# One kernel, one change: who makes the low half of a split weight tile in the mixer's input projections

## The chip, the cores and the metric

The kernel runs on one core of one Trainium2 chip. The metric is the time of one execution on the device in microseconds (us). Five engines work side by side and meet at semaphores: TensorE (PE in the profile; its weight loads are the row PEld), VectorE (DVE), ScalarE (ACT), GpSimd (POOL) and SyncE (SP). SP issues nearly all loads from DRAM; POOL issues a few transfers through a queue of its own. The transfers of all queues are carried by the core's 16 DMA engines.

## The reference: what is computed

A diffusion backbone of two layers over 256 latent and 256 context tokens of width 1024. All is float32. Each layer has three parts, each with its own RMS norm, shift, scale and gate:

```python
x = add_residual(x, swiglu(modulate(x, ...), ffn_w_in[l, 0], ffn_w_out[l, 0]), ...)
h = modulate(x, ...); hc = modulate(xc, ...)
rq, rk, rv, rg, dq, dk, dv, gates = jnp.split(h @ w_in, SPLIT_POINTS, axis=-1)   # same for hc
# retention heads from rq, rk, rv, rg; differential attention heads from dq, dk, dv
y = (g_a * ret_out + g_b * diff_out) @ w_out
x = add_residual(x, y, ...)
x = add_residual(x, swiglu(modulate(x, ...), ffn_w_in[l, 1], ffn_w_out[l, 1]), ...)
```

The change touches the product `h @ w_in`, which is 1024 x 8192 weights per layer. In the second layer the context tokens need only some of its columns, since their output is not used any more.

## The kernel before, in words

TensorE multiplies in a reduced format (float32r). To keep float32 accuracy every operand is split into a high half (the value rounded to float32r) and a low half (what the rounding left), and every product is three matmuls (`mm3`, lines 301 to 303): high times high, high times low, low times high. In the transposed projections (`projT`, `ps<-h,w` in the profile) a weight tile's low half is first read by line 303, in the plain ones (`proj`, `ps<-w,h`) by line 302. The matmul ahead of it needs the high half alone.

Weights come from DRAM as tiles of 128 x 1024 float32 (512 KB), issued by SP into a ring of four buffers (`rawp`, line 121). `split` (line 125) turns one such tile into a pair of halves in a ring of five buffers (`wp`): ScalarE writes the high half with a copy (line 128), VectorE writes the low half as source minus high half (line 129). A raw buffer is free again when both have read it; a `w` buffer is free when TensorE has done its last matmul with it.

The mixer of a layer (`mixer`) runs 32 projection blocks, each of 256 columns of `w_in` and thus of two weight tiles. `proj_w` loads and splits the two; `projT_c` and `proj_c` do the matmuls for the latent and the context tokens, 48 matmuls for each of the two. In the second layer 18 of the 32 blocks are for the latent tokens alone. A tile framework orders each engine's instructions at build time, puts the attention and retention work between the projections, and adds the semaphores. Each engine then runs its list strictly in order: an instruction that waits holds up all that stand behind it. Around the mixer stand the feed-forward stages (`ffn`) and the norms: `norm_xn` (line 248 scales by a factor from POOL, lines 232 to 235), `norm_q` (lines 259 to 267: transposes on TensorE, shift and scale on ScalarE). The evictions of the projections (`rotate`, `ev_diff`, lines 504 to 532) run on VectorE and ScalarE.

Of the kernel before, what the change touches and what calls it, by code (L numbers as in the profile page):

```python
# [12 lines left out]
F32R = mybir.dt.float32r  # L13
BF16 = mybir.dt.bfloat16
AF = mybir.ActivationFunctionType
ALU = mybir.AluOpType
AX = mybir.AxisListType

P = 128
# [13 lines left out]
def build(ctx, tc, a):  # L33
    nc = tc.nc
# [3 lines left out]
    pool = nc.gpsimd  # L38
# [4 lines left out]
    wp = ctx.enter_context(tc.tile_pool(name="wp", bufs=5))  # L43
# [73 lines left out]
    def load(src, halves=(0, 1), pl=rawp, nm="raw"):  # L117
        rs = []
        for j in halves:
            r = pl.tile([P, 1024], F32, tag=nm, name=nm)  # L120
            nc.sync.dma_start(r, src[:, j * 1024:(j + 1) * 1024])
            rs.append(r)
        return rs

    def split(src, pin=False):
        keep = tc.keep_in_program_order if pin else (lambda z: z)
        w = wp.tile([P, 2, 1024], F32R, tag="w", name="w")
        keep(nc.scalar.copy(w[:, 0, :], src))  # L128
        keep(dve.tensor_tensor(out=w[:, 1, :], in0=src, in1=w[:, 0, :], op=ALU.subtract))  # L129
        return w  # L130

    cs = {}
# [172 lines left out]
    def fin_w(l, i, f, halves=(0, 1), pin=False):  # L305
        return [split(r, pin) for r in load(a["fin"][l, i, f], halves)]
# [10 lines left out]
    def ffn(l, i, st, AB, fetch, pairs, side, nside, after=None, out=None):  # L317
# [51 lines left out]
        def fout_w(f2):  # L369
            r = load(a["fout"][l, i, f2])  # L370
            ws = [split(r[0]), split(r[1])]
            if f2 < NP - 2:
                gt = hp.tile([P, 2, 2, 512], F32R, tag="h", name="gs")
                gs = [gt[:, 0], gt[:, 1]]
            else:
                gs = [slot([P, 2, 512], F32R) for _ in range(2)]
            for j in range(2):
                gsrc = g[f2][:, j, :N]
                nc.scalar.copy(gs[j][:, 0, :N], gsrc)
                dve.tensor_tensor(out=gs[j][:, 1, :N], in0=gsrc, in1=gs[j][:, 0, :N], op=ALU.subtract)  # L380
            slots.put(g[f2])
            return ws, gs
# [30 lines left out]
    def mixer(l, st, AB, fetch, after):  # L413
# [42 lines left out]

        def proj_w(b):
            r = load(a["win"][l, b])
            return [split(r[0]), split(r[1])]

        def proj_c(ws, c, ev):
            b0 = bank()
# [14 lines left out]
        def proj(b, pairs, ev):  # L477
            ws = proj_w(b)
            for c in pairs:
                proj_c(ws, c, ev)  # L480

        def projT(b, pairs, ev):
            ws = proj_w(b)
            for c in pairs:
                projT_c(ws, c, ev)
# [303 lines left out]
        def diff_blocks(u):  # L789
            KH = [slot([P, 2, 512], F32R) for _ in range(2)]  # L790
            KL = [slot([P, 2, 512], F32R) for _ in range(2)]
            Q = [slot([P, 2, 512], F32R) for _ in range(2)]
            dv = slot([P, 4, 256])
            ek, eq = ev_diff(KH, KL), ev_diff(Q, None)
            if u == 0:
                wk, wq = proj_w(16), proj_w(12)
                projT_c(wk, LAT, ek)
                norm_pair(CTX, AB, h)
                projT_c(wq, LAT, eq)
                projT_c(wk, CTX, ek)  # L800
                if not last:
                    projT_c(wq, CTX, eq)
                K.update(mixer_consts())
            else:
                projT(16 + u, BOTH, ek)
                projT(12 + u, QP, eq)
            proj(20 + u, BOTH, ev_V(dv))
            flush()
            defer(f"d{u}", diff_attn(u, KH, KL, Q, dv), 2 * NQ + 3, 4 * NQ + LAG)
# [57 lines left out]
        def wo_w(u):  # L867
            r = load(a["wout"][l, u])
            return [split(r[0]), split(r[1])]
# [8 lines left out]
        for u in range(n0):  # L878
            w = wo_w(u)
# [3 lines left out]
        w = sum((wo_w(u) for u in range(n0, 4)), [])  # L883
# [145 lines left out]
```

## Time and profile before

| | |
|---|---|
| median of 3 runs | 2225.74 us (2221.16 to 2225.74) |
| the profiled execution's own time | 2223.86 us |
| its span in the profile | 2222.1 us |
| mean granted TensorE clock | 0.993 of full |
| TensorE busy | 2173.7 us (98%) |
| VectorE busy | 1381.6 us (62%) |
| ScalarE busy | 863.5 us (39%) |
| POOL busy | 130.7 us (6%) |
| first layer's mixer, projections | about 407 to 879 us |
| second layer's mixer, projections | about 1664 to 1994 us |

The share of an engine is an average over stages. What matters for a change in one stage is which wait ends last there, so the timeline of that stage is read beside the totals. Idle time of an engine that nobody waits for costs nothing.

### The profile page before, as it was taken

Reading aid. Unit: us, or ns where it says so; the run is one execution under the profiler, and the core shown is the slowest. Engines: PE = TensorE matmul, PEld = TensorE weight load, DVE = VectorE, ACT = ScalarE, POOL = GpSimd, SP = SyncE. Lnnn points to the kernel's source line nnn. Section 1 sums busy time; section 2 is a strip of 40 time slices with the busy share of each in tenths; the row PEclk is TensorE's granted clock in tenths of the full one; section 3 lists DMA queues with packets and bytes.
Section 4 is the critical chain, followed back from the end, with each engine's and each line's share of the span. In section 5 each row is a group of like instructions: output and inputs, shape, how many; then the busy total and the mean of one; then the engine's idle time right before and its main releaser. Section 6 shows DMA issues by size and latency. Waiting matters only on the chain. (4 is left out here: it accounts for less than half of the span.)

```text
span 2222.1 us, 32737 instructions
## 1 busy us (share of the span) xinstructions
PE 2173.7 (98%) x13190; PEld 1932.0 (87%) x13190; DVE 1381.6 (62%) x2240; ACT 863.5 (39%) x1379; POOL 130.7 (6%) x248
## 2 busy tenths in 40 slices
PE   7999999999999999999999999999999999998998
PEld 4888888899999999888888888888889999997997
DVE  3799542777767664587234269844348777767554
ACT  3322232645355432432233252223236545445443
POOL 1000000200100010200000020000010010001000
PEclk9999999999999999999999999999999999999999
DMA  9577432212122223266223227853213222345553
GB/s 339 188 253 251 168 114 95 69 68 80 66 77 77 81 84 115 77 212 217 102 95 133 95 100 255 293 187 114 95 64 109 103 88 101 129 154 180 187 184 133
DMA packets 85081, 307.31 MB, mean 138 GB/s; under 512 B 9969, under 2 KB 10049, under 8 KB 84929
## 3 DMA queue, kind: packets, MB, share of 16 engines
q1 hardware_dynamic: 81648, 295.73, 38.2%
q0 software_dynamic: 2848, 8.43, 1.4%
q8 instruction: 103, 1.69, 0.3%
q10 hardware_dynamic: 432, 1.06, 0.1%
q14 instruction: 50, 0.40, 0.1%
HBM read 304.10 MB, written 1.09 MB: 137 GB/s over the span
## 5 line engine op out<-in xcount | busy, mean ns | idle before, releaser
L129 DVE TENSOR_TENSOR w<-raw,w 128x1024 fp32r<-128x1024 f32 x408 | 497.3, 1221 | 461.4 <-ACT w L128 459.9
L301 PE MATMUL ps<-h,w 128*128 128x256 f32 (+1 forms) x2144 | 712.5, 334 | 3.2 <-DVE h L266 2.9
L302 PE MATMUL ps<-h,w 128*128 128x256 f32 (+1 forms) x2144 | 712.9, 333 | 0.0
L303 PE MATMUL ps<-h,w 128*128 128x256 f32 (+1 forms) x2144 | 712.1, 333 | 0.5 <-DVE w L129 0.5
L128 ACT CAST w<-raw 128x1024 fp32r<-128x1024 f32 x408 | 427.5, 1052 | 678.9 <-PE ps L303 606.1
L301 PEld LDWEIGHTS ps<-h,w 128*128 128x128 f32 x2144 | 407.6, 191 | 47.1 <-DVE h L266 7.3
L302 PEld LDWEIGHTS ps<-h,w 128*128 128x128 f32 x2144 | 408.3, 190 | 40.4 <-issue 0.8
L303 PEld LDWEIGHTS ps<-h,w 128*128 128x128 f32 x2144 | 407.8, 190 | 39.2 <-DVE w L129 1.1
L301 PE MATMUL ps<-w,h 128*128 128x256 f32 x1088 | 308.9, 284 | 0.0
L302 PE MATMUL ps<-w,h 128*128 128x256 f32 x1088 | 308.1, 283 | 0.0
L303 PE MATMUL ps<-w,h 128*128 128x256 f32 x1088 | 307.8, 283 | 0.0
L146 DVE CUSTOM_DVE_ANT_0 jd<-ada,r 128x1024 bf16<-128x1024 f32 x224 | 273.4, 1220 | 15.0 <-DMA ada<-wada_dram 10.0
L301 PEld LDWEIGHTS ps<-w,h 128*128 128x128 f32 x1088 | 208.6, 192 | 0.4
L302 PEld LDWEIGHTS ps<-w,h 128*128 128x128 f32 x1088 | 208.7, 192 | 0.3
L303 PEld LDWEIGHTS ps<-w,h 128*128 128x128 f32 x1088 | 208.6, 192 | 0.0
L301 PE MATMUL ps<-w,gs 128*128 128x512 f32 x504 | 196.2, 389 | 0.0
L302 PE MATMUL ps<-w,gs 128*128 128x512 f32 x504 | 196.1, 389 | 0.0
L303 PE MATMUL ps<-w,gs 128*128 128x512 f32 x504 | 196.1, 389 | 0.0
L330 ACT ACTIVATE t<-ps 128x512 f32<-128x512 f32 (+1 forms) x88 | 47.9, 544 | 252.7 <-PE ps L303 252.7
L331 DVE TENSOR_TENSOR r<-ps,t 128x512 f32<-128x512 f32 (+1 forms) x88 | 54.7, 622 | 94.5 <-PE ps L303 65.3
L301 PEld LDWEIGHTS ps<-w,gs 128*128 128x128 f32 x504 | 94.6, 188 | 19.7
L302 PEld LDWEIGHTS ps<-w,gs 128*128 128x128 f32 x504 | 94.6, 188 | 19.7
(172 smaller groups left out, 2171.5 us busy)
## 6 DMA issues: line engine op xcount, KB each, us to landing
raw<-fin_dram SPq DMA_DIRECT2D x176, 512.0 KB, 4.1
ada<-wada_dram SPq DMA_DIRECT2D x128, 512.0 KB, 4.8
raw<-win_dram SPq DMA_DIRECT2D x128, 512.0 KB, 3.6
raw<-fout_dram SPq DMA_DIRECT2D x88, 512.0 KB, 3.5
r<-wada_dram SPq DMA_DIRECT2D x16, 512.0 KB, 10.3
raw<-wout_dram SPq DMA_DIRECT2D x16, 512.0 KB, 3.6
r<-scr POOLq DMA_DIRECT2D x10, 512.0 KB, 4.6
r<-cc_dram SPq DMA_DIRECT2D x7, 512.0 KB, 5.8
```

The source lines that it names most:

```text
L128: keep(nc.scalar.copy(w[:, 0, :], src))
L129: keep(dve.tensor_tensor(out=w[:, 1, :], in0=src, in1=w[:, 0, :], op=ALU.subtract))
L146: dve.tensor_tensor_reduce(out=junk, in0=r[j], in1=cs[c], scale=1.0, scalar=0.0, op0=ALU.mult, op1=ALU.add, accum_out=out[:, c, 2 * u + j: ...
L301: mm(o, lhsT=wH, rhs=xH, start=start, stop=False)
L302: mm(o, lhsT=wH, rhs=xL, start=False, stop=False)
L303: mm(o, lhsT=wL, rhs=xH, start=False, stop=stop)
L330: act(sg[:, :N], ab[0][:, :N], AF.Silu)
L331: dve.tensor_tensor(out=g[f // 2][:, f % 2, :N], in0=ab[1][:, :N], in1=sg[:, :N], op=ALU.mult)
```

## The change

A second way to split is added and used for the weights of `w_in` alone. ScalarE writes the high half as before. ScalarE then writes the negated source, rounded the same way, into the low half's place. POOL issues a transfer from the raw tile onto the low half's place that adds: source plus the negated high half. VectorE has no part in these 128 tiles (64 in each layer). The tiles of the feed-forward stages and of `w_out` are split as before.

```diff
+    def split_acc(src):
+        w = wp.tile([P, 2, 1024], F32R, tag="w", name="w")
+        nc.scalar.copy(w[:, 0, :], src)
+        nc.scalar.mul(w[:, 1, :], src, -1.0)
+        pool.dma_start(w[:, 1, :], src, accum_op=ALU.add)
         return w
...
         def proj_w(b):
             r = load(a["win"][l, b])
-            return [split(r[0]), split(r[1])]
+            return [split_acc(r[0]), split_acc(r[1])]
```

Line numbers behind the new function are 7 higher in the changed kernel: 527 becomes 534, 232 becomes 239. The new instructions are lines 134 (copy), 135 (negated copy) and 136 (adding transfer).

The change moves instructions on three engines. First ScalarE in the second layer, at the second tile of a block that follows a block for the latent tokens alone (`w_15109` before, `w_15188` now; r and ps are the targets and sources of the evictions). Before:

```order
L527 CAST r12_14892<-ps5_14974 64x2x256
L128 CAST w_15109<-raw_15104 128x1024
L531 CAST r12_14892<-ps5_14974 64x2x256
L532 COPY r4_14894<-r4_14894 64x2x256
L527 CAST r13_14893<-ps5_14974 64x2x256
L128 CAST w_15216<-raw_15212 128x1024
```

Now:

```order
L534 CAST r12_14966<-ps5_15050 64x2x256
L134 CAST w_15188<-raw_15182 128x1024
L538 CAST r12_14966<-ps5_15050 64x2x256
L539 COPY r4_14968<-r4_14968 64x2x256
L534 CAST r13_14967<-ps5_15050 64x2x256
L135 ACTIVATE w_15188<-raw_15182 128x1024
L538 CAST r13_14967<-ps5_15050 64x2x256
```

The negated copy stands three evictions behind the copy of the same tile, where the next tile's copy stood before.

Second, ScalarE in the second layer some 130 us later (`w_16689` before, `w_16792` now). Before:

```order
L128 CAST w_16689<-raw_16684 128x1024
L527 CAST r1_16463<-ps4_16554 64x2x256
L527 CAST r1_16463<-t2_16538 64x2x256
L531 CAST r1_16463<-t2_16538 64x2x256
L527 CAST r2_16464<-t2_16538 64x2x256
```

Now:

```order
L134 CAST w_16792<-raw_16786 128x1024
L534 CAST r1_16561<-t2_16638 64x2x256
L538 CAST r1_16561<-t2_16638 64x2x256
L534 CAST r2_16562<-t2_16638 64x2x256
L539 COPY r4_16563<-r4_16563 64x2x256
L538 CAST r2_16562<-t2_16638 64x2x256
L539 COPY r14_16564<-r14_16564 64x2x256
L534 CAST r1_16561<-ps4_16654 64x2x256
L135 ACTIVATE w_16792<-raw_16786 128x1024
```

Here seven evictions stand between a tile's copy and its negated copy.

Third, POOL at the start of the first layer's mixer, where the factors of the norms are made (pm, pr). Before:

```order
L235 TENSOR_TENSOR pr_2905<-pm_2902,cneg_98 128x1
L232 TENSOR_SCALAR pm_2942<-ss_2933 128x1
L233 TENSOR_SCALAR pm_2942<-ss_2933,pm_2942 128x1
L235 TENSOR_TENSOR pr_2945<-pm_2942,cneg_98 128x1
L232 TENSOR_SCALAR pm_3047<-ss_3042 128x1
```

Now:

```order
L242 TENSOR_TENSOR pr_2905<-pm_2902,cneg_98 128x1
L239 TENSOR_SCALAR pm_2942<-ss_2933 128x1
L136 DMA w_2965<-raw_2959 128x1024
L240 TENSOR_SCALAR pm_2942<-ss_2933,pm_2942 128x1
L242 TENSOR_TENSOR pr_2945<-pm_2942,cneg_98 128x1
L136 DMA w_2973<-raw_2969 128x1024
L136 DMA w_2977<-raw_2971 128x1024
L239 TENSOR_SCALAR pm_3051<-ss_3046 128x1
```

Adding transfers stand among the norm factors, in the order in which their tiles are made.

## Rows read from the trace of the kernel before

**Rows 1.** The page, part 1: busy us (share), xinstructions, by engine.

```profile
PE 2173.7 (98%) x13190; PEld 1932.0 (87%) x13190; DVE 1381.6 (62%) x2240; ACT 863.5 (39%) x1379; POOL 130.7 (6%) x248
```

**Rows 2.** Stretches: length, busy by engine, granted clock, DMA share, GB/s.

```profile
1660.00:1990.00 330.00, 326.70 (x2626) 318.58 (x2626) 250.69 (x443) 174.09 (x288) 24.74 (x44) 1.00 0.33 111
430.00:880.00 450.00, 444.05 (x3599) 434.22 (x3598) 303.62 (x620) 200.83 (x377) 31.14 (x61) 1.00 0.24 81
2000.00:2050.00 50.00, 42.35 (x266) 38.81 (x266) 34.87 (x48) 26.86 (x43) 7.76 (x12) 0.90 0.51 177
400.00:450.00 50.00, 47.55 (x353) 45.55 (x352) 41.94 (x80) 33.60 (x61) 8.34 (x13) 0.97 0.26 88
```

**Rows 3.** Waits of PE: waited for, us in total, times, longest.

```profile
PE ps L259 <- DVE t L248: 16.5, 12, 6.2
...
PE ps L303 <- DVE w L129: 0.5, 2, 0.2
```

**Rows 4.** Groups: busy us, mean ns | idle before, releaser.

```profile
L129 DVE TENSOR_TENSOR w<-raw,w 128x1024 fp32r<-128x1024 f32 x408 | 497.3, 1221 | 461.4 <-ACT w L128 459.9
...
L128 ACT CAST w<-raw 128x1024 fp32r<-128x1024 f32 x408 | 427.5, 1052 | 678.9 <-PE ps L303 606.1
```

**Rows 5.** Timeline (start us, us, instruction, idle before), first layer, 829 to 846 us.

```profile
829.56 1.05 ACT L128 CAST w<-raw 128x1024 fp32r<-128x1024 f32 x1 [4.84 <-PE ps L303]
...
845.32 0.28 PE L302 MATMUL ps<-w,h 128*128 128x256 f32 x1
```

**Rows 6.** DMA queue q1 (packets, MB, share); issues (KB each, us to landing).

```profile
q1 hardware_dynamic: 81648, 295.73, 38.2%
...
raw<-win_dram SPq DMA_DIRECT2D x128, 512.0 KB, 3.6
...
r<-wada_dram SPq DMA_DIRECT2D x16, 512.0 KB, 10.3
...
r<-scr POOLq DMA_DIRECT2D x10, 512.0 KB, 4.6
```

**Rows 7.** Timeline, ACT and PE, second layer, 1739 to 1744 us.

```profile
1739.17 1.05 ACT L128 CAST w<-raw 128x1024 fp32r<-128x1024 f32 x1
...
1741.96 1.05 ACT L128 CAST w<-raw 128x1024 fp32r<-128x1024 f32 x1
...
1743.59 0.28 PE L302 MATMUL ps<-w,h 128*128 128x256 f32 x1
```

**Rows 8.** Timeline, ACT and PE, start of the first layer's mixer.

```profile
405.01 2.95 ACT L128 CAST w<-raw 128x1024 fp32r<-128x1024 f32 x3
...
408.91 0.39 PE L303 MATMUL ps<-h,w 128*128 128x256 f32 x1
```

**Rows 9.** Timeline, ACT and PE, second layer, 1871 to 1878 us.

```profile
1871.65 0.62 ACT L527 CAST r<-t 64x512 fp32r<-64x512 f32 x1 [0.81 <-DVE t L509]
...
1877.37 0.28 PE L302 MATMUL ps<-w,h 128*128 128x256 f32 x1
```

**Rows 10.** Timeline, ACT and PE, first layer, 433 to 439 us.

```profile
433.53 1.05 ACT L128 CAST w<-raw 128x1024 fp32r<-128x1024 f32 x1 [6.65 <-PE ps L303]
434.48 1.26 ACT L527 CAST r<-t 64x512 fp32r<-64x512 f32 x2
435.76 0.58 ACT L527 CAST r<-ps 64x512 fp32r<-64x512 f32 x1
...
438.37 0.28 PE L302 MATMUL ps<-w,h 128*128 128x256 f32 x1
```

**Rows 11.** Timeline, ACT and PE, second layer, 1680 to 1685 us.

```profile
1681.73 2.85 ACT L263 ACTIVATE t<-ps,adaB,adaA 128x256 f32<-128x256 f32 x6
...
1680.12 0.28 PE L302 MATMUL ps<-w,h 128*128 128x256 f32 x1
```

**Rows 12.** Timeline, PE: two places where it stood [idle before <-releaser].

```profile
424.66 0.50 PE L301 MATMUL ps<-h,w 128*128 128x256 f32 x2 [1.77 <-DVE h L266]
...
2022.23 1.09 PE L259 MATMUL ps<-ident,t 128*128 128x128 f32 x4 [6.15 <-DVE t L248]
```

More of the change, by code (lines that the diff above doesn't have):

```diff
@@ L129, in split @@
         keep(dve.tensor_tensor(out=w[:, 1, :], in0=src, in1=w[:, 0, :], op=ALU.subtract))
+        return w
+    def split_acc(src):
[3 more added lines that the diff above has]
+        pool.dma_start(w[:, 1, :], src, accum_op=ALU.add)
         return w
```

## The prediction

> **What bounds the kernel now.** I read the shares of the engines first: TensorE is busy for 98% of the span, VectorE for 62%, ScalarE for 39% and POOL for 6% [rows 1]. Next come the stretches of the two mixers: in 430 to 880 us TensorE is idle for 450 - 444.05 = 5.95 us, in 1660 to 1990 us for 330 - 326.7 = 3.3 us, at the full granted clock [rows 2]. So in the stages that change, TensorE sets the pace, and all that could be won by making its operands sooner is some 9 us. The waits of TensorE say the same: it waited for VectorE's low half of a weight tile twice, 0.5 us in all; its longest waits are for the norms [rows 3]. VectorE's 408 subtractions of 1221 ns were hidden, and in 460 of their 461 us of idle time VectorE waited for ScalarE's copy. ScalarE's copies in turn waited 606 us for TensorE [rows 4]: the ring of five `w` buffers was full, and a copy starts when a buffer comes free. What matters is therefore the distance from a copy's end to the first matmul that reads the low half. The usual case in the first layer is wide: one copy ends at 829.56 + 1.05 = 830.6 and its low half is read at 845.32, 14.7 us later [rows 5]. A few places are narrow, and these decide.
>
> **The change part by part.** It takes 128 x 1.221 us = 156 us from VectorE [rows 4]. That work lay beside TensorE's, so by itself it is worth nothing but a part of the 9 us above. It adds 128 negated copies to ScalarE; with the 1.052 us of the plain copy [rows 4] that is 135 us, on an engine with 174 busy us in 330 [rows 2]. It adds 128 transfers to POOL's queue. These are in the way of little: POOL works 25 us in 330 [rows 2], and the instructions behind a waiting transfer are norm factors which in most places come some us later anyway.
>
> What goes on the path is the age at which a low half is ready. Before: the copy's end plus 1.22 us. Now: the copy's end, then the negated copy (1.05 us, later if evictions stand between), then 0.1 us for the semaphore and the adding transfer.
>
> No adding transfer is in the trace, so I bound its time from issue to landing. Below: 3.6 us, a 512 KB load on the hardware queue. Above: 10.3 us, the same size in the crowd at the start. Nearest: 4.6 us, 512 KB on POOL's own queue [rows 6]. It must read the target as well as the source. The hardware queue kept 16 engines busy for 0.382 x 2222 = 849 us with 295.73 MB, that is 1.5 us for 512 KB [rows 6]; I add that once, as for a second reading, to 4.6 and take 6.1 us. With 0.1 us, the low half is ready 6.2 us after the negated copy (3.7 to 10.4).
>
> The nearest transfer of that size took 4.6 us. The Trainium skill, in "DMA: Bandwidth & Descriptors" (Anatomy of one DMA), fits POOL's transfers with 2.0 us plus the bytes at 436 GB/s: 3.2 us for 512 KB, and as an estimate 4.4 us for 1 MiB, if both readings count. By it each stall below is 1.7 us shorter and the result some 12 us lower. The row is longer than the rule, so I stay with the row.
>
> The narrow places, each tile found by counting the rows of the order in the trace, with the times of before:
>
> - Second layer, 1739 to 1744 us. The negated copy takes the slot that the next tile's copy had, 1741.96, and ends at 1743.0. Ready at 1749.2; read at 1743.59 [rows 7]. Stall 5.6 us. The same pattern comes once more, 82 us later: 5.6 us. In both the preceding block is for the latent tokens alone, so the buffer came free only some 7 us ahead.
> - Start of the first layer's mixer. The first of three copies from 405.01 ends at 406.1, the negated copy at 407.1, ready 413.3, read at 408.91 [rows 8]: 4.4 us. The second layer starts in the same pattern, with 4.6 us.
> - 1871 us: seven evictions (six of 0.62 to 0.63 us, one of 0.58) now stand between copy and negated copy. From 1871.65 they end at 1876.1, the negated copy at 1877.1, ready 1883.3. TensorE read at 1877.37 and now has four matmuls ahead of that, 4 x 0.12 = 0.5 us (444 us for 3599 matmuls [rows 2]), so at 1877.9 [rows 9]: 5.4 us.
> - 433 us: copy from 433.53, three evictions to 436.4, negated copy to 437.4, ready 443.6. Read at 438.37, now 16 matmuls later, 440.3 [rows 10]: 3.3 us.
> - 1680 us: the copy now stands behind the context norm's ScalarE work, which ended at 1684.6; without the copy that stood ahead of it 1683.5. Copy and negated copy end at 1685.6, ready 1691.8. Read at 1680.12, now 62 matmuls (7.4 us) later, 1687.6 [rows 11]: 4.2 us.
> - Three more tiles fall short by 0.4 to 1.0 us: 2.4 us.
>
> A stall at one place delays TensorE's release of buffers with it, so stalls at different places add up; tiles whose copies lie close behind a stall are covered by it. Sum: 5.6 + 5.6 + 4.4 + 4.6 + 5.4 + 3.3 + 4.2 + 2.4 = 35.5 us.
>
> The clock adds to it. After TensorE stood for 6.15 us at 2016 us [rows 12], the stretch 2000 to 2050 shows a mean granted clock of 0.90 [rows 2]: a fifth of it at 1.2 instead of 2.4 GHz, worth 0.10 x 50 = 5 us. After a gap of 1.77 us at 423 us [rows 12] the mean in 400 to 450 is 0.97 [rows 2], 1.5 us. The seven stalls of 3.3 to 5.6 us lie between, and I take the middle, 3.25 us each: 23 us. Against it, the gap at 423 us was a wait for VectorE's norm work; with TensorE later by then, it and its clock go: -3 us.
>
> Sum: 35.5 + 23 - 3 = 55 us on the profiled execution's 2223.9 us, 2279 us. The median of the runs is 1.9 us above that execution: 2281, said as **2280 us**.
>
> Bounds: at 3.7 us after the negated copy the seven stalls shrink by 2.5 us each to 15.6, the small ones go, with 1.5 us of clock each: 15.6 + 10.5 - 3 = 23 us, 2249. At 10.4 us each grows by 4.2 us to 62.5, some 20 further tiles with 6.2 to 10.4 us to spare come short by 2 us on average, half of them covered by a stall ahead (20 us), the clock costs 5 us each: 62.5 + 20 + 35 - 3 = 115 us, 2341.
>
> **The rivals.**
>
> *The DMA engines become the bound of the second layer's mixer.* They are busy for 0.33 x 330 = 109 us there now [rows 2]. 63 tiles at twice 1.5 us add 189 us: 298 of 330, close already, and my forecast holds only while that fits. At three times (source and target read, target written, each paced alone) they need 109 + 63 x 4.5 = 393 us: the stretch grows by 63 us, and the first layer (0.24 x 450 + 284 = 392 of 450) keeps its three or four stalls with longer landings, some 15 us plus clock 10. 2226 + 88 = 2314 us; a still slower adder goes beyond 2340. For it: each tile already has 5.2 us on the average there. Against it: no row shows such a price. 20%.
>
> *The stalls are smaller than counted.* The order on TensorE may leave other work at hand, or VectorE's relief brings the evictions between the two copies forward by 1 to 2 us, and stalls of about 2 us each without much clock remain: 7 x 2 + 3 = 17 us, 2243 us. 12%.
>
> *The transfer is hidden anyway.* Then the time is that of before, 2226 us. For it: 14.7 us of distance in the usual case [rows 5]. Against it: the seven places. 6%.
>
> *Faster: VectorE's relief decides.* The 9.3 us of idle TensorE in the mixers and the two gaps of [rows 12] are largely waits for VectorE's norms, evictions and softmax; with 156 us less to do VectorE would serve these first and the mixers lose up to 10 us: 2216 us. It decides only if the low half is ready within some 1 us of the negated copy at the narrow places, against 3.6 us for any 512 KB transfer [rows 6]. 4%.
>
> **How the numbers follow.** Forecast (2250 to 2310): 58%; DMA bound: 20%; smaller stalls: 12%; hidden: 6%; faster: 4%. The range leaves out the hidden and the faster case, the lower part of the small one and what lies beyond a DMA bound of 2350: 2235 to 2350. About 0.2% (4.5 us) is what a measurement here can tell from no change: slower by more 0.89, within 0.07, faster 0.04.
>
> **What would show it.** In the changed profile TensorE should wait for the adding transfer of `w` at about seven places, two at the mixers' starts, one near 433, one each near 1680, 1739, 1821 and 1871 (each shifted by the stalls ahead), 3 to 6 us each, with a granted clock below 1.00 behind them. The landing of the adding transfers should be near 6 us. VectorE's busy time should fall by 156 us and ScalarE's rise by 135 us. The feed-forward stages should not change. I am wrong if TensorE's waits for `w` are spread over all blocks of the second layer (DMA bound), if the landing is outside 3.6 to 10.3 us, or if TensorE's idle time does not rise.

## The result and the profile after

The changed kernel takes 2279.95 us (median, 2271.94 to 2282.75), the kernel before on the same chip 2223.47 us (four runs; 2225.74 was the median of the first three): a ratio of 1.0253, 95% interval 1.0236 to 1.0269. The change costs 56.5 us. The profiled execution after took 2282.64 us, of which 2280.9 are the span.

Page of the changed kernel, part 1, answering [rows 1], and parts 3, 5 and 6, answering [rows 4, 6]:

```profile
PE 2191.5 (96%) x13190; PEld 1948.4 (85%) x13190; DVE 1243.7 (55%) x2112; ACT 978.5 (43%) x1507; POOL 237.3 (10%) x376
...
q1 hardware_dynamic: 81648, 295.73, 37.1%
q0 software_dynamic: 21280, 75.55, 17.5%
...
L134 ACT CAST w<-raw 128x1024 fp32r<-128x1024 f32 x128 | 134.0, 1047 | 123.5 <-PE ps L310 96.2
L136 POOL DMA_DIRECT2D w<-raw x128 | 112.7, 882 | 659.1 <-ACT w L135 507.5
...
L135 ACT ACTIVATE w<-raw 128x1024 fp32r<-128x1024 f32 x128 | 135.6, 1059 | 0.3
...
raw<-win_dram SPq DMA_DIRECT2D x128, 512.0 KB, 4.9
w<-raw POOLq DMA_DIRECT2D x128, 512.0 KB, 5.8
```

TensorE does the same 13190 instructions. Its idle time in the span rose from 2222.1 - 2173.7 = 48.4 us to 89.4, that is 41 us, and its busy time by 17.8 us: the same matmuls at a lower clock. POOL's queue q0 had 1.4% of the engines' time before; the rest, 0.161 of 2281 us, is some 367 us for 128 adding transfers, 2.9 us of all 16 engines each, against the 1.5 us of a load of that size. A load of `win` takes 4.9 us to land where it took 3.6 [rows 6].

The stretches, answering [rows 2] (first mixer, feed-forward stages between, second mixer; columns as there):

```profile
400.00:904.00 504.00, 485.24 (x3827) 471.59 (x3826) 267.23 (x605) 279.68 (x484) 92.45 (x136) 0.99 0.60 145
904.00:1668.00 764.00, 759.52 (x3544) 635.96 (x3543) 410.40 (x570) 237.77 (x337) 34.81 (x63) 1.00 0.43 148
1668.00:2066.00 398.00, 365.02 (x2752) 349.33 (x2751) 199.02 (x402) 244.60 (x376) 79.59 (x114) 0.97 0.74 183
```

The loss lies in the mixers: TensorE is idle for 33 us of the second one's 398, at a mean granted clock of 0.97. The two feed-forward stages between them take 1.7 and 1.6 us more than before.

TensorE's waits, answering [rows 3]:

```profile
PE ps L266 <- DVE t L255: 15.3, 12, 6.2
PE ps L309 <- DMA w<-raw: 13.6, 8, 3.0
PE ps L649 <- ACT t L646: 9.7, 6, 2.3
PE ps L308 <- DVE t L719: 8.0, 5, 2.7
PE ps L310 <- DMA w<-raw: 6.8, 3, 3.5
...
PE ps L644 <- DVE rc L628: 4.5, 3, 4.0
```

Two kinds make the difference. TensorE waits directly for adding transfers, 13.6 + 6.8 = 20.4 us at 11 places. And it waits longer for work of ScalarE and VectorE that has nothing to do with weights: the attention's evictions (line 646; 1.0 us before), the retention's split into halves on VectorE (line 719; 2.4 before) and the softmax factors (line 628; not in the list before): 22.2 us, 18.8 more than before. 20.4 + 18.8 makes 39 of the 41 us.

The first kind at one place of the second mixer (timeline, ScalarE, POOL and TensorE; start, length, instruction, idle time before it):

```profile
1855.50 1.06 ACT L135 ACTIVATE w<-raw 128x1024 fp32r<-128x1024 f32 x1
...
1856.97 0.88 POOL L136 DMA_DIRECT2D w<-raw  x1 [12.55 <-ACT w L135]
...
1858.57 0.60 PE L308 MATMUL ps<-w,h 128*128 128x256 f32 x2
1861.56 0.38 PE L309 MATMUL ps<-w,h 128*128 128x256 f32 x1 [2.38 <-DMA w<-raw]
```

The negated copy ends at 1856.56, POOL starts the issue 0.4 us later, and TensorE reads the low half 5.0 us after the negated copy; it stood for 2.38 us.

The second kind, 70 us earlier (timeline, ScalarE, POOL, SyncE and TensorE):

```profile
1778.32 1.05 ACT L134 CAST w<-raw 128x1024 fp32r<-128x1024 f32 x1 [2.22 <-PE ps L310]
...
1780.73 0.88 POOL L136 DMA_DIRECT2D w<-raw  x1 [6.75 <-ACT w L135]
...
1782.51 0.33 SPq L121 DMA_DIRECT2D raw<-win_dram  x1
...
1784.30 0.90 POOL L690 DMA_DIRECT2D t<-strip_dram  x1
...
1786.58 0.33 SPq L121 DMA_DIRECT2D raw<-win_dram  x1
1788.28 1.05 ACT L134 CAST w<-raw 128x1024 fp32r<-128x1024 f32 x1 [1.83 <-DMA raw<-win_dram]
...
1793.19 0.71 ACT L700 ACTIVATE W<-t,lg,lg 128x384 f32<-128x384 f32 x1 [2.90 <-DMA t<-strip_dram]
1793.80 0.67 ACT L625 ACTIVATE t<-ps,nb 128x512 f32<-128x512 f32 x1
...
1796.95 0.52 PE L644 MATMUL ps<-ident,t 128*128 128x128 f32 x3 [4.04 <-DVE rc L628]
```

Three things meet. The loaded half copied at 1778.32 is also the source of the adding transfer issued at 1780.73, so its buffer is given to the next load only at 1786.58, 8.3 us after the copy began. Before, the copy at 1739.17 [rows 7] was followed by that load at 1741.51, 2.3 us later. For the 59 tiles of the second mixer whose buffer goes to another tile of `w_in`, the median time from a copy's start to the issue of the next load into its buffer went from 2.4 to 9.4 us. Next, the load issued at 1782.51 took 5.8 us on the crowded engines, and ScalarE, which works in order, stood 1.83 us for it. Last, the decay strip, a 192 KB transfer on POOL's queue, was issued at 1784.30, right behind an adding transfer that had waited for its negated copy, and reached ScalarE at 1793.19. The exponentials (line 625) stood behind it, and TensorE waited 4.04 us for what follows from them. In the kernel before the strip was issued at 1735.55 and used at 1760.95, 25.4 us later; the eight strip transfers landed in 2.7 us (median) there and in 5.9 us now. Timelines of the kernel before, SyncE, POOL and ScalarE:

```profile
1741.51 19.27 SPq L121 DMA_DIRECT2D raw<-win_dram  x7
...
1735.55 0.62 POOL L683 DMA_DIRECT2D t<-strip_dram  x1 [6.18 <-DVE t L509]
...
1760.95 0.70 ACT L693 ACTIVATE W<-t,lg,lg 128x384 f32<-128x384 f32 x1
```

ScalarE's waits (same columns as TensorE's) show the last two over the whole span; the kernel before has no such wait for `win`, and waited 2.1 us once for the strip:

```profile
ACT w L134 <- DMA raw<-win_dram: 21.7, 11, 5.2
...
ACT W L700 <- DMA t<-strip_dram: 14.1, 4, 6.8
```

### The profile page after: what moved, and what is told of

It is laid out like the page before. It is cut to its first block, busy times and chain, and to the rows that moved or that the text cites. A ratio compares the mean times of both kernels' runs of the same rounds, so it can differ in the third digit from the quotient of the medians.

```text
span 2280.9 us, 33065 instructions
## 1 busy us (share of the span) xinstructions
PE 2191.5 (96%) x13190; PEld 1948.4 (85%) x13190; DVE 1243.7 (55%) x2112; ACT 978.5 (43%) x1507; POOL 237.3 (10%) x376
## 3 DMA queue, kind: packets, MB, share of 16 engines
q0 software_dynamic: 21280, 75.55, 17.5%
q10 hardware_dynamic: 432, 1.06, 0.1%
## 5 line engine op out<-in xcount | busy, mean ns | idle before, releaser
L129 DVE TENSOR_TENSOR w<-raw,w 128x1024 fp32r<-128x1024 f32 x280 | 341.9, 1223 | 388.7 <-ACT w L128 386.0
L309 PE MATMUL ps<-w,h 128*128 128x256 f32 x1088 | 311.5, 287 | 13.6 <-DMA w<-raw 13.6
L309 PEld LDWEIGHTS ps<-w,h 128*128 128x128 f32 x1088 | 211.3, 194 | 15.9 <-DMA w<-raw 15.4
L308 PEld LDWEIGHTS ps<-w,h 128*128 128x128 f32 x1088 | 211.2, 194 | 0.7
L310 PEld LDWEIGHTS ps<-w,h 128*128 128x128 f32 x1088 | 211.4, 194 | 0.0
L136 POOL DMA_DIRECT2D w<-raw x128 | 112.7, 882 | 659.1 <-ACT w L135 507.5
L135 ACT ACTIVATE w<-raw 128x1024 fp32r<-128x1024 f32 x128 | 135.6, 1059 | 0.3
## 6 DMA issues: line engine op xcount, KB each, us to landing
r<-wada_dram SPq DMA_DIRECT2D x16, 512.0 KB, 10.2
```

The costliest lines, as they stand in the source:

```text
L135: nc.scalar.mul(w[:, 1, :], src, -1.0)
L136: pool.dma_start(w[:, 1, :], src, accum_op=ALU.add)
L308: mm(o, lhsT=wH, rhs=xH, start=start, stop=False)
L309: mm(o, lhsT=wH, rhs=xL, start=False, stop=False)
L310: mm(o, lhsT=wL, rhs=xH, start=False, stop=stop)
```

## The experiments

The kernel before took 2221.4 to 2222.0 us in these comparisons. Each mixer's stage is read from TensorE's first norm transpose (line 259 before, 266 after) ahead of it to the first of the next stage, in the profiled execution; "mixers" is the sum of both against the kernel before. A stage is thus read from one execution, and the runs of one kernel spread over 4 to 12 us. A loss named below is a median's distance from the kernel before of its own comparison.

| kernel | median us | ratio, 95% | first | second | mixers |
|---|---|---|---|---|---|
| before | 2223.5 | | 520.8 | 369.7 | |
| the change | 2280.0 | 1.0236–1.0269 | 535.4 | 410.7 | +55.6 |
| e1 VectorE adds | 2227.9 | 1.0018–1.0042 | 520.1 | 372.9 | +2.5 |
| e4 first layer only | 2237.7 | 1.0052–1.0082 | 536.1 | 368.2 | +13.8 |
| e3 six `w` | 2263.1 | 1.016–1.0198 | 525.6 | 402.5 | +37.6 |
| e5 six `raw` | 2266.2 | 1.0192–1.0223 | 532.0 | 400.5 | +42.0 |
| e12 strip once | 2268.4 | 1.0194–1.024 | 530.1 | 403.6 | +43.2 |
| e7 six `w`, strip once | 2254.0 | 1.0136–1.0167 | 526.0 | 394.0 | +29.5 |
| e9 six `w`, five `raw`, strip once | 2267.1 | 1.0185–1.0219 | 526.9 | 383.5 | +19.9 |
| e6 no addition | 2237.7 | 1.0054–1.0087 | 525.5 | 379.3 | +14.3 |
| e11 half the columns | 2252.1 | 1.0109–1.0146 | 529.4 | 390.9 | +29.8 |
| e10 other order | 2279.9 | 1.0243–1.0283 | 536.0 | 408.6 | +54.1 |

**e1: is it the transfer, or ScalarE's second copy?**

```diff
-        pool.dma_start(w[:, 1, :], src, accum_op=ALU.add)
+        dve.tensor_tensor(out=w[:, 1, :], in0=src, in1=w[:, 1, :], op=ALU.add)
```

> The changed kernel, but VectorE adds the source onto the negated copy; there is no adding transfer. ScalarE still makes two copies for each tile. Theory (about half of the loss is TensorE waiting for the adding transfer at narrow places, the other half is ScalarE and POOL held up by transfers that share the DMA engines; ScalarE's 135 us of extra copies cost little by themselves): the low half is 1.05 us later than before at the narrow places, so 2228 to 2233 us, ratio 1.002 to 1.005. Rival 1 (ScalarE's extra copies hold up the evictions): 2245 us or more, ratio over 1.010.

2227.88 us. The 128 negated copies stay (135.6 us of ScalarE) and VectorE has its work back; some 6 us remain of the loss. So the transfer in VectorE's place costs about 50 us and the longer way over ScalarE some 6.

**e2: traffic without a reader.** The kernel before, with 128 adding transfers onto one tile that nothing reads.

```diff
+    jt = cst.tile([P, 1024], F32, name="jt")
...
+            for z in r:
+                pool.dma_start(jt, z, accum_op=ALU.add)
```

> The kernel before with its own split, and beside it 128 adding transfers from the same raw tiles onto a tile that nothing reads (one buffer less in the ring for the modulation weights to make room for it). Nobody on TensorE waits for these transfers. Theory: the second half of the loss alone, the loads, the strip transfers and ScalarE behind them: 2235 to 2250 us, ratio 1.005 to 1.012, with no wait of TensorE for a transfer onto w. Rival 2 (sharing the DMA engines is the whole loss): 2265 us or more, ratio over 1.019. If the waits at the narrow places were all of it: 2223 to 2228 us.

2338.83 us: far above the theory's range and inside rival 2's "2265 us or more", but no clean measurement of it, since with one target each transfer waits for the one before it. Waits of POOL:

```profile
POOL jt L463 <- DMA jt<-raw: 448.3, 90, 8.1
POOL jt L463 <- DMA raw<-win_dram: 359.9, 31, 78.0
```

POOL's norm factors and the buffers of the loads stand behind these waits. It shows only that transfers that nobody reads can cost more than the change, through the queue and the buffers that they hold.

**e4: the first layer alone.**

```diff
+            f = split_acc if l == 0 else split
+            return [f(r[0]), f(r[1])]
```

> The change in the first layer alone (64 of the 128 tiles); the second layer splits as before. From the two traces the first layer's mixer grew by 14.6 us and the second's by 42.2 us. Theory (narrow places and crowded DMA engines lie mostly in the second layer, whose blocks for the latent tokens alone leave half the time for a tile): 2235 to 2242 us, ratio 1.005 to 1.009. Rival (a cost by tile, the same in both layers): 2250 to 2254 us, ratio 1.0125.

2237.72 us, as the theory expected. The two mixers' losses are separate: +15.3 us in the first stage here as with the full change (+14.6), none in the second (-1.5). Per tile the second mixer costs 2.8 times as much.

**e3 and its control e8: more lead for the low half.**

```diff
-    adap = ctx.enter_context(tc.tile_pool(name="adap", bufs=4))
-    wp = ctx.enter_context(tc.tile_pool(name="wp", bufs=5))
+    adap = ctx.enter_context(tc.tile_pool(name="adap", bufs=2))
+    wp = ctx.enter_context(tc.tile_pool(name="wp", bufs=6))
```

> The changed kernel with six instead of five buffers for split weight tiles (two instead of four for the modulation weights to make room). Theory: copies at the narrow places in the second layer start one half block, 3 to 6 us, sooner, so TensorE's waits for the adding transfer fall from 20 us to under 8 us and the clock drops behind them go; 2245 to 2262 us, ratio 1.010 to 1.017. Rival 2 (sharing of the DMA engines is the whole loss): no change against the changed kernel, 2275 to 2285 us.

> Control: the kernel before with six weight buffers and two conditioning buffers. All theories expect no change within 0.3%: 2216 to 2228 us. If it is over 2230, the two conditioning buffers cost time in the runs that use them.

2263.08 us, 1 us above the expected range; the same buffers in the kernel before: 2224.04 us (ratio 1.0001 to 1.0019), so the buffers by themselves change it by some 2 us. Waits of TensorE in e3:

```profile
PE ps L644 <- DVE rc L628: 21.4, 3, 8.1
...
PE ps L308 <- DVE t L719: 9.2, 4, 2.9
```

The direct waits fell from 20.4 to 1.9 us, but the waits behind the softmax factors rose from 4.5 to 21.4: the wait moved to work that stands behind ScalarE. With the direct waits nearly gone, some 42 of the 56 us of loss stay. The seven narrow places are not the whole cause.

**e5 to e7: held buffers, shared engines, the strip.** e5 gives two more buffers to the loads:

```diff
-    rawp = ctx.enter_context(tc.tile_pool(name="rawp", bufs=4))
-    adap = ctx.enter_context(tc.tile_pool(name="adap", bufs=4))
+    rawp = ctx.enter_context(tc.tile_pool(name="rawp", bufs=6))
+    adap = ctx.enter_context(tc.tile_pool(name="adap", bufs=2))
```

> The change with six buffers for loaded weight halves instead of four (and two for the conditioning weights instead of four). Theory H (held buffers): the adding transfer reads the loaded half, so its buffer is given to the next load 8.3 to 8.9 us after the high copy starts, where it was 2.3 to 2.5 us; loads start that much later, ScalarE's copies wait for them (21.7 us in 11 waits) and the evictions and exponentials behind them come late. With six buffers those waits fall under 8 us and the time to 2260 to 2272 us; TensorE's direct waits for the low half stay near 20 us. Theory T (shared DMA engines: a load takes 5.3 us in the second mixer where it took 3.6): the buffers do nothing, 2276 to 2286 us, ScalarE's waits for loads stay over 15 us.

2266.17 us, as theory H expected: ScalarE no longer waits for `win` (21.7 us in the change), TensorE's direct waits are 21.2 us. TensorE's waits in e5:

```profile
PE ps L309 <- DMA w<-raw: 14.4, 8, 3.0
...
PE ps L310 <- DMA w<-raw: 6.8, 2, 3.6
...
PE ps L649 <- ACT t L646: 2.1, 3, 1.5
```

The wait for the evictions fell from 9.7 to 2.1 us. The held buffers were worth some 12 us (give or take 5, by the two intervals).

e6 takes the addition from the transfer:

```diff
-        pool.dma_start(w[:, 1, :], src, accum_op=ALU.add)
+        pool.dma_start(w[:, 1, :], src)
```

> The change with a transfer that copies and does not add, so the low half is the weight itself (the subtraction of the rounded copy is left out). The engines do one pass less per tile if the addition needs the second read. Theory T: 16 DMA engines' time per transfer falls from 2.9 to about 1.5 us, loads take about 4.2 us again, landing of the transfer 4 to 4.5 us instead of 5.8, time 2245 to 2262 us. Theory H: a buffer is still held some 6.5 to 7.5 us, so most of the late copies stay: 2265 to 2276 us. If the addition costs nothing: 2280 us, landing 5.8.

2237.73 us, less than either theory said. Page of e6, parts 3 and 6:

```profile
q0 software_dynamic: 21280, 75.55, 10.1%
...
raw<-win_dram SPq DMA_DIRECT2D x128, 512.0 KB, 4.2
w<-raw POOLq DMA_DIRECT2D x128, 512.0 KB, 3.9
```

With the same bytes the queue takes 10.1% instead of 17.5%: 1.5 us per transfer, like a load. The landing falls from 5.8 to 3.9 us. Theory H gave 2265 at least; it took the hold of the buffer for a cost beside the traffic, while a shorter transfer shortens hold, landing and crowd at once. The addition alone makes some 41 of the 56 us.

e7 is e3 with the strip loaded once at the start:

```diff
-            strip = tmp2([P, 384])
-            pool.dma_start(strip, a["strip"])
+            strip = strip0
```

> Six weight buffers, two conditioning buffers (2263.1 us was measured for that alone), and the decay strip loaded once at the start instead of eight times on GpSimd's queue. Theory S (strip transfers behind adding transfers on GpSimd's queue make the decay exponentials late): the TensorE gap of 8.1 us near 1770 goes with the 1.7 us of half clock behind it, 2250 to 2256 us. Theory H or T (ScalarE waits for loads there anyway; the strip is only what it meets last): 2260 to 2264 us, the gap stays over 5 us.

2254.01 us, the time theory S gave, but its gap did not go: it fell from 8.1 to 5.8 us, over the 5 us that theories H and T gave. TensorE's and ScalarE's waits in e7 (lines are 2 higher):

```profile
PE ps L646 <- DVE rc L630: 18.1, 3, 6.6
```

```profile
ACT w L136 <- DMA raw<-win_dram: 30.7, 12, 4.1
```

In e3 ScalarE stood 1.52 us for the strip ahead of that gap. This wait is gone; the four waits for loads ahead of it, 1.3 to 2.9 us each, are still there.

**e12: the strip once, otherwise the change** (three conditioning buffers).

> The change with the decay strip loaded once at the start instead of eight times on GpSimd's queue (three conditioning buffers instead of four). Theory S: the 4.0 us gap of TensorE near 1797 and the half clock behind it go, and with GpSimd's queue shorter by 0.9 us some of the waits behind VectorE's factors: 2268 to 2276 us. If ScalarE's copies come late from the loads alone: 2277 to 2284 us and a gap of over 2.5 us stays there.

2268.37 us, as theory S expected. The 4.0 us gap is gone and that wait is 3.8 us (4 times, at most 1.9). Taking eight transfers of 192 KB off the queue is worth some 10 us (give or take 6, by the two intervals), more than that one gap. In the profiled execution 5 us are won in the first mixer's stage, where the largest gap that goes is 2 us. The strip loaded once was not tried in the kernel before; there TensorE has no wait for it.

**e9: all of it together.** Six `w`, five `raw`, the strip once, and one conditioning buffer, since nothing else made room.

> Six weight buffers, five buffers for loaded halves, the decay strip loaded once, one conditioning buffer. If three separable causes (direct waits for the low half, held load buffers, the strip's queue) make the loss: ScalarE's waits for loads fall from 30.7 us under 12, TensorE's waits behind the decay factors from 18.1 us under 6, the time to 2236 to 2246 us. If the shared DMA engines alone set it, buffers only shift the place: 2250 to 2256 us as with six weight buffers and the strip. The one conditioning buffer could cost some us between the mixers (waits for the conditioning transfers), which the waits would show.

2267.12 us: missed, as a total and in both waits named. Waits of TensorE in e9:

```profile
PE ps L646 <- DVE rc L630: 8.2, 3, 3.0
PE ps L213 <- DVE adag L209: 7.7, 2, 4.7
...
PE ps L311 <- DVE w L131: 5.4, 1, 5.4
...
PE ps L311 <- DMA w<-raw: 2.8, 3, 1.3
```

The conditioning (`adag`) and the feed-forward weights ahead of the mixer came late: outside the mixers this kernel lost 26 us, where e7 with two conditioning buffers and e5 with six `raw` lost less than 1. So this is put down to the one buffer; no run has it alone. In the mixers +55.6 fell to +19.9 us, so room to wait takes back two thirds of the loss there. It does so although the second mixer's transfers are no faster: the engines are 75% busy there, the loads of `win` land in 5.5 us and the adding transfers in 7.4 (medians). ScalarE still waited 14.0 us for `win`. What holds the last 20 us is not told apart further.

**e10: the transfer 1 us earlier.**

```diff
-        nc.scalar.copy(w[:, 0, :], src)
         nc.scalar.mul(w[:, 1, :], src, -1.0)
         pool.dma_start(w[:, 1, :], src, accum_op=ALU.add)
+        nc.scalar.copy(w[:, 0, :], src)
```

> The change with ScalarE's two instructions in the other order: negated copy and transfer first, then the high copy, so each transfer starts 0.95 us earlier. Theory D (at the narrow places the lone path copy, negated copy, transfer of 5.0 us sets the stall): TensorE's 11 direct waits fall by about 1 us each, 20.4 to 9 to 13 us, one or two stretches of half clock go, 2264 to 2273 us. Rival: TensorE needs the high half that much later and the engines are crowded, so the wait only changes its name: 2276 to 2284 us.

2279.88 us; the rival was right. Waits of TensorE in e10:

```profile
PE ps L644 <- DVE rc L628: 11.3, 3, 5.5
PE ps L309 <- DMA w<-raw: 9.3, 7, 1.6
...
PE ps L310 <- DMA w<-raw: 7.9, 4, 3.8
```

The direct waits fell by 3 us, and 7 us came back behind the softmax factors.

**e11: half the columns, VectorE adds the others.**

```diff
+        pool.dma_start(w[:, 1, :512], src[:, :512], accum_op=ALU.add)
+        dve.tensor_tensor(out=w[:, 1, 512:], in0=src[:, 512:], in1=w[:, 1, 512:], op=ALU.add)
```

> The transfer adds 512 of the 1024 columns of each half, VectorE adds the other 512 onto the negated copy. Theory T (the share of the DMA engines that the adding transfers take, 2.9 us each): half of it is 1.45 us, as with the transfer that did not add, so about its time, 2235 to 2246 us, with a share of some 10% for the queue and loads landing in about 4.3 us in the second mixer. Theory L (the fixed part of each transfer's way, issue to landing, sets the stalls and the hold of the buffers): it stays near 4 us at the lone places, 2252 to 2268 us.

2252.1 us, at the lower edge of theory L; T's share of the queue came true, its time did not. Page of e11:

```profile
q0 software_dynamic: 21280, 42.00, 10.2%
...
w<-raw POOLq DMA_DIRECT2D x128, 256.0 KB, 4.0
```

The engines' time per transfer is that of e6 (10.2% and 10.1%), the landing too (4.0 and 3.9 us median), and yet it is 14 us slower. Direct waits are 10.8 us here and 7.7 in e6; the shortest landing is 3.2 and 2.8 us. But the two kernels differ in VectorE as well: here it makes 128 half additions and stood 108.6 us for the negated copies ahead of them, and TensorE's waits behind VectorE in the attention, the retention and the norms' halves are some 10 us longer than in e6. What part of the 14 us is the transfer's is not told apart. Half of the loss for half of the work: the mixers' +29.8 against +55.6.

## Why the prediction came out

2280 us was predicted and 2279.95 measured, in the range. The direction and the direct mechanism were right. That the sum meets the median so closely is luck: a term that was too large covered one that was missing. Of the 58.8 us between the profiled executions, 20.4 are direct waits (35.5 predicted), 17.8 longer matmuls (23 predicted) and 18.8 waits behind ScalarE and VectorE that the prediction did not have.

- **TensorE sets the pace; the relief of VectorE is worth nothing.** Right as far as the runs go. VectorE lost its 156 us (group L129 fell from 497.3 to 341.9; its total by 138, as overlaps count once), and TensorE's longest wait for VectorE, for the norms, went only from 16.5 to 15.3 us. The negated copies took 135.6 us of ScalarE (its total rose by 115, for the same reason); with VectorE's work unchanged they cost some 6 us in e1. No run has the relief of VectorE alone.
- **The seven narrow places.** Six of the seven show a stall, all smaller than predicted: 3.20 us at the first mixer's start (predicted 4.4), 1.65 near 443 (3.3), 3.45 at the second mixer's start (4.6), 2.42 (5.6), 2.38 (5.6) and 2.96 (5.4). The 1680 place stood 0.30 us (4.2). Three more tiles stood 1.06, 1.64 and 1.18 us (2.4 in all were put down for such), but at the end of the second mixer and for transfers that took 13.8, 9.2 and 6.0 us to land: these are places of a crowd, not narrow ones.
- **The step that failed: "take 6.1 us" from issue to landing, 35.5 us of stalls.** At the seven places the transfer lands in 4.5 to 4.9 us and the low half is read 5.0 to 5.4 us after the negated copy, not 6.2 (POOL's start took 0.4 us of it, where 0.1 was put). The direct stalls are 20.4 us, 15 too few. The 1.5 us for the second reading was about right: e6's plain transfer over the same way lands in 2.8 us at the least, the adding one in 4.5. What was too large is the base, 4.6 us from another kind of transfer: one row in DRAM spread over all partitions. The shorter way from the negated copy to the reading explains 8 of the 17 us by which the seven places fell short of their 33.1. The other 9 come from the reader, which stood further behind the negated copy than was counted: 2.6 us where 0.6 was taken near 1739 and 1821, 4.7 where 2.0 was taken near 1680, 2.1 where 0.8 was taken near 1871. At the first two, TensorE has some 14 more matmuls (1.7 us) ahead of the reading than before, which the prediction counted at other places but not there. The Trainium skill's fit ("DMA: Bandwidth & Descriptors", Anatomy of one DMA), counted for two readings, gave an estimate of 4.4 us, with which the lone transfers agree; the median over all 128 is 5.8 us, and two, with 10.6 and 13.8 us, lie beyond the upper bound of 10.3.
- **The clock.** 23 us predicted; TensorE's busy time rose by 17.8 us with the same instructions. Right in kind: behind the stand of 2.38 us shown above, the granted clock is 0.79 in 1860 to 1865 us and 0.87 in the next 5 us, where it was 1.00 in the 5 us ahead: part of each is run at 1.2 instead of 2.4 GHz (stretches of the changed kernel, columns as in [rows 2]):

```profile
1855.00:1860.00 5.00, 4.17 (x34) 3.83 (x32) 4.37 (x7) 4.94 (x7) 0.88 (x1) 1.00 0.35 69
1860.00:1865.00 5.00, 3.44 (x21) 3.44 (x22) 1.83 (x3) 4.72 (x6) 1.69 (x2) 0.79 0.94 166
1865.00:1870.00 5.00, 5.00 (x39) 5.00 (x39) 0.00 (x0) 0.59 (x1) 0.86 (x1) 0.87 1.05 297
```

- **The 3 us taken off.** The gap near 423 us did not go: it is 1.05 us now where it was 1.77.
- **What was missing: 18.8 us behind ScalarE.** This term was put at nothing: the text took "the instructions behind a waiting transfer" for norm factors that come later anyway, and looked at the reader of the transfer alone. It did not ask when the source comes free (the `raw` buffer, reloaded after 9.4 instead of 2.4 us), nor what else uses POOL's queue (the strip). e5 and e12 put these at some 12 and 10 us, with the clock behind the stalls.
- **The DMA-bound rival** was half there. Its price, three units of 1.5 us per transfer, is wrong: 2.9 us is two, as in the forecast. The second mixer's engines are 74% busy, not full; but at that share loads land in 5.3 us there where they took 3.6. e6, with less of their time taken, gives most of the loss back, though it shortens the transfer itself as well; and e9 takes back two thirds of the mixers' loss with the engines as busy as before. That fits a share that costs through longer landings, as far as no buffer covers them; how much of the loss is the share's alone is not shown.
- **Hidden, smaller stalls, faster:** the first and the last are refuted by the result. The smaller stalls (2 us each) were nearer the truth at the seven narrow places, 2.3 us on average, than the forecast was, and other work of TensorE ahead of the reading is part of it, as that rival had it; but its time lacks the waits behind ScalarE and the clock.

## What to carry to other kernels

A transfer put in place of an instruction has four parties: the reader of its target, the next user of its source buffer, whoever shares its queue, and the engines' other transfers; follow all four, since more buffers or an earlier start for one move part of the wait to the next (e3, e10). When ScalarE, whose list runs in order, waits for a late load, what stands behind it is late, and TensorE's wait then carries a name far from the cause, as at 1797 us above. A sum that agrees with the clock is no proof of its terms: read each one off the new trace.

## What the runs showed of the hardware

- An adding transfer from one on-chip tile to another takes 2.9 us of all 16 DMA engines for 512 KB, the plain one 1.5 (e6); adding 256 KB takes as much as copying 512 KB (e11).
- From issue to landing the shortest adding transfer of 512 KB took 4.5 us, the plain one 2.8, the adding one of 256 KB 3.2. POOL's issue itself takes 870 ns (median) for the adding one, of 512 KB or of 256 KB (e11), and 540 for the plain one of 512 KB (e6).
- With the engines 74% busy, 512 KB loads on the hardware queue took 5.3 us (median) in the second mixer, at 33% 3.6 (the kernel before).
